# A decoder layer in fp32 on one core: FFN products in Strassen's seven-product form, all mixers first

## The chip, the cores and the metric

The kernel runs on one core of a Trainium2 chip. The metric is the device time of one execution in microseconds. The engines are PE (TensorE, matrix multiplication, with its weight loads PEld), DVE (VectorE), ACT (ScalarE), POOL (GpSimd) and SP (SyncE, which here issues nearly all transfers). Each works through its own instructions in order and waits on semaphores for the others.

## The reference

One layer on a sequence of 2048 tokens with 1024 features; hidden size of the FFN 4096; all float32. Cut to what matters:

```python
mod = silu(c) @ w_ada + b_ada                    # six vectors of 1024
shift1, scale1, gate1, shift2, scale2, gate2 = split(mod, 6)
h = rms_norm(x, g_mix) * (1 + scale1) + shift1
proj = h @ w_in                                  # gMLP u | v, then q, k, v: 1792 columns
out_a = chunked_sgu(gelu(proj[:, :1024]), w_spatial, b_spatial)      # chunks of 128 tokens
out_b = sliding_window_sink_attention(q, k, v, sinks, positions)     # window 128, 8 q and 2 kv heads
x = x + gate1 * (concat(out_a, out_b) @ w_out)
h2 = rms_norm(x, g_ffn) * (1 + scale2) + shift2
x = x + gate2 * (square(relu(h2 @ w_ff1)) @ w_ff2)
y = rms_norm(x, g_final)
```

## The kernel before

Activations are kept feature-major, 128 features on the partitions, and the sequence is cut into four slabs of T = 512 tokens. Every fp32 matrix product is made of three passes: each factor is split into a rounded part (`hi`, made by ACT, L253 for weights) and the rest (`lo`, made by DVE, L255), and `mm3` (L267 to L269) issues hi·hi, hi·lo and lo·hi into the same bank. Weights stream from DRAM in blocks of 128x1024: `w_next` keeps two blocks ahead in the order of the list `order`, each loaded by SP into one of three `raw` buffers.

A slab goes through `in_vu` (gMLP projection and gate), `in_qkv`, `attention`, `out_proj`, `ffn` and `final_norm`. `attention` has eight units (four blocks of 128 queries, two key heads), each in four stages: `stage_q` splits the queries; `stage_p` makes the scores (`sc`, L503) and their softmax in `pr` (DVE L510, L525, ACT's exponentials); `stage_t` transposes them (`tpp`, L534), splits them into `pc` (ACT L536, DVE L537) and masks them on POOL (`pp`, L541, L543); `stage_o` multiplies by the values (`ov`, L558) and copies out (`os`, ACT L561). `ffn` has eight chunks of 512 hidden features: four groups of 24 matmuls for the first product, then eight output groups of 12 for the second, added to `x2` (L634).

Generators set the program's order: `weave(main, side)` takes a step of `side` after each step or two of `main`. While slab s is in `ffn`, `attention` of slab s+1 and the statistics of slab s+2 are woven into it; `attention` of slab 0, which has no FFN before it, is skewed by stages and woven into the gMLP projections of slabs 0 and 1. The last slab's last chunk goes in halves of the columns, so that one half is normalised under the other. A scheduler then fixes each engine's order of instructions, with hand-written `issue_after` bounds.

The three places that decide what stands beside what:

```python
weave(chain(h_build(1, rb, hn), in_vu(1, hn, nxt)), zipped(att, ada), per=2)   # slab 0
...
side.append(attention(s + 1, nxt, False))
...
weave(main, chain(*side), every=2)                                             # main = ffn(s, st, h2)
```

## Time and profile before

| | |
|---|---|
| runs | 2143.32, 2145.67, 2146.58 us; median 2145.67 |
| span of the profiled execution | 2142.5 us (no other time is recorded for it) |
| PE busy | 2050.3 us, 9670 matmuls |
| DVE busy | 1296.7 us |
| ACT busy | 966.9 us |
| POOL busy | 256.7 us |
| transferred | 240.27 MB, mean 112 GB/s |

Busy times are sums over one profiled execution. PE's matmuls are pipelined, so that its busy time says when it was occupied and not that it ran at its peak; PEclk is the clock granted to TensorE, 1.00 being full speed. Marks of stages on PE: the first output projection begins at about 262 us, the first FFN at about 372 us.

### The profile page before, as it was taken

The page shows a single profiled execution, that of the slowest core. Times are in us where ns is not written, and L with a number is a line of the kernel's source. Part 1 is how long each engine was busy: PE and PEld are TensorE (multiplying, and loading weights), DVE is VectorE, ACT ScalarE, POOL GpSimd, SP SyncE. Part 2 cuts the span into 40 slices and gives each one's busy share as a digit, 9 for nine tenths or more (in the row PEclk, how much of TensorE's full clock was granted, in tenths as well). Part 3 has the DMA queues.
Part 4 walks back from the last instruction along what each step waited for, and adds up shares of the span by engine and source line. Part 5 has one row for each costly group of instructions (what it writes and reads, how often), then busy time and mean ns, then how long its engine had stood idle before and what let it go on. Part 6 is the DMA issues. An engine that isn't in the chain of part 4 may idle for free.

```text
span 2142.5 us, 25614 instructions
## 1 busy us (share of the span) xinstructions
PE 2050.3 (96%) x9670; PEld 1715.7 (80%) x9670; DVE 1296.7 (61%) x2068; ACT 966.9 (45%) x1642; POOL 256.7 (12%) x234
## 2 busy tenths in 40 slices
PE   5878898999999999999999999999999999999997
PEld 4777776888888888888887889888888888888886
DVE  8698768656563577655564577665554456444445
ACT  3555654544443443544453434444444243333334
POOL 5742253100000000100000000010000000000001
PEclk9978999999999999999999999999999999999998
DMA  9442172322233352322233362222222323322331
GB/s 333 151 145 64 55 245 93 107 89 80 98 128 99 111 186 89 99 89 89 89 103 113 99 206 89 89 89 98 82 93 92 118 94 123 113 99 89 99 98 60
DMA packets 81372, 240.27 MB, mean 112 GB/s; under 512 B 9904, under 2 KB 12080, under 8 KB 81248
## 3 DMA queue, kind: packets, MB, share of 16 engines
q1 hardware_dynamic: 80128, 237.91, 33.6%
q8 instruction: 76, 1.25, 0.2%
q0 software_dynamic: 1120, 0.72, 0.1%
q14 instruction: 48, 0.39, 0.1%
HBM read 230.01 MB, written 8.59 MB: 111 GB/s over the span
## 4 chain that ended last, share of the span: by engine, by line
PE 83%; DVE 7%; POOL 3%; ACT 2%; DMA 2%; issue 2%; SPq 0%; DVEq 0%; POOLq 0%; ACTq 0%
PE mm L267 26%; PE mm L269 25%; PE mm L268 25%; POOL acc L163 1%; PE sc L503 1%; PE ov L558 1%; PE mm L429 1%; PE mm L431 1%; PE mm L430 1%; DVE pr L510 1%; DVE wlo L255 1%; DMA xt<-in_x_dram 1%; DMA adap<-in_wada_dram 1%; PE tpp L534 1%; DMA raw<-in_win_dram 1%
## 5 line engine op out<-in xcount | busy, mean ns | idle before, releaser
L253 ACT ACTIVATE whi<-raw 128x1024 fp32r<-128x1024 f32 x344 | 363.9, 1059 | 819.3 <-PE mm L268 776.6
L255 DVE TENSOR_TENSOR wlo<-raw,whi 128x1024 fp32r<-128x1024 f32 x335 | 421.0, 1258 | 358.0 <-ACT whi L253 318.9
L267 PE MATMUL mm<-h,whi 128*128 128x512 f32 x1344 | 526.9, 394 | 12.0 <-ACT h L227 11.6
L269 PE MATMUL mm<-h,wlo 128*128 128x512 f32 x1344 | 526.8, 392 | 2.1 <-DVE wlo L255 1.6
L268 PE MATMUL mm<-h,whi 128*128 128x512 f32 x1344 | 526.1, 392 | 0.3 <-DVE h L228 0.3
L268 PE MATMUL mm<-a,whi 128*128 128x512 f32 (+1 forms) x1056 | 403.1, 384 | 0.0
L269 PE MATMUL mm<-a,wlo 128*128 128x512 f32 (+1 forms) x1056 | 402.6, 383 | 0.0
L267 PE MATMUL mm<-a,whi 128*128 128x512 f32 (+1 forms) x1056 | 395.5, 386 | 3.2 <-DVE x L634 3.1
L267 PEld LDWEIGHTS mm<-h,whi 128*128 128x128 f32 x1344 | 255.4, 190 | 65.0 <-ACT h L227 12.5
L269 PEld LDWEIGHTS mm<-h,wlo 128*128 128x128 f32 x1344 | 253.6, 189 | 55.4 <-DVE wlo L255 3.8
L268 PEld LDWEIGHTS mm<-h,whi 128*128 128x128 f32 x1344 | 254.0, 189 | 52.5 <-DVE h L228 1.3
L267 PEld LDWEIGHTS mm<-a,whi 128*128 128x128 f32 x1056 | 197.9, 188 | 47.7 <-DVE x L634 7.3
L269 PEld LDWEIGHTS mm<-a,wlo 128*128 128x128 f32 x1056 | 198.4, 188 | 39.0
L268 PEld LDWEIGHTS mm<-a,whi 128*128 128x128 f32 x1056 | 198.5, 188 | 37.5
L634 DVE SCALAR_TENSOR_TENSOR x<-mm,mod,x 128x512 f32<-128x512 f32 x192 | 140.0, 749 | 117.3 <-PE mm L269 116.6
L541 POOL TENSOR_SCALAR_AFFINE_SELECT pp<-pc 128x1024 fp32r<-128x1024 f32 x30 | 33.1, 1105 | 845.4 <-DVE pc L537 845.4
L615 DVE TENSOR_TENSOR a<-r,a 128x512 fp32r<-128x512 f32 x128 | 88.4, 692 | 63.5 <-ACT a L614 63.5
L199 POOL TENSOR_TENSOR rs<-ms,mhalf 128x4 f32<-128x4 f32 (+1 forms) x13 | 15.3, 1177 | 859.1 <-DVE ms L197 859.1
L429 PE MATMUL mm<-whi,h 128*128 128x256 f32 x256 | 75.4, 302 | 8.0 <-ACT vf L417 4.3
L614 ACT ACTIVATE a<-r 128x512 fp32r<-128x512 f32 x128 | 80.6, 631 | 5.2
L612 ACT ACTIVATE r<-r 128x512 f32<-128x512 f32 x128 | 80.8, 632 | 3.5
L634 DVE SCALAR_TENSOR_TENSOR x2p<-mm,mod,x2p 128x512 f32<-128x512 f32 x56 | 40.8, 749 | 67.0 <-PE mm L269 67.0
(185 smaller groups left out, 2482.5 us busy)
## 6 DMA issues: line engine op xcount, KB each, us to landing
raw<-in_w_dram SPq DMA_DIRECT2D x256, 512.0 KB, 3.5
raw<-in_win_dram SPq DMA_DIRECT2D x56, 512.0 KB, 4.2
xt<-in_x_dram SPq DMA_DIRECT2D x80, 256.0 KB, 3.1
raw<-in_wout_dram SPq DMA_DIRECT2D x32, 512.0 KB, 3.5
ada<-in_wada_dram SPq DMA_DIRECT2D x16, 512.0 KB, 8.1
adar<-in_wada_dram SPq DMA_DIRECT2D x32, 256.0 KB, 3.9
adap<-in_wada_dram SPq DMA_DIRECT2D x16, 512.0 KB, 5.1
out_dram<-y SPq DMA_DIRECT2D x24, 256.0 KB, 2.9
```

The source lines that it names most:

```text
L163: pool.tensor_tensor(out=acc, in0=acc, in1=raw, op=ALU.add)
L253: act.activation(out=hi, in_=raw, func=AF.Copy)
L255: ins = eng.tensor_tensor(out=lo, in0=raw, in1=hi, op=ALU.subtract)
L267: pe.matmul(out=out, lhsT=wh, rhs=h[:, 0], start=first, stop=False)
L268: pe.matmul(out=out, lhsT=wh, rhs=h[:, 1], start=False, stop=False)
L269: pe.matmul(out=out, lhsT=wl, rhs=h[:, 0], start=False, stop=last)
L429: pe.matmul(out=ov[:, b], lhsT=h[k][:, 0, cols], rhs=hi, start=k == 0, stop=False)
L541: pool.affine_select(out=pp, in_=pc, pattern=[[0, 8], [-1, P]], compare_op=ALU.is_gt, fill=0.0, base=0, channel_multiplier=1)
L612: act.activation(out=r, in_=r, func=AF.Square)
L614: act.activation(out=a[:, 0], in_=r, func=AF.Copy)
L615: dve.tensor_tensor(out=a[:, 1], in0=r, in1=a[:, 0], op=ALU.subtract)
L634: dve.scalar_tensor_tensor(out=x2[d], in0=outs[dd], scalar=mod[:, 5 * KT + d:5 * KT + d + 1], in1=x2[d], op0=ALU.mult, op1=ALU.add)
```

## The change

Two slabs form a pair. Each FFN product is a 2x2 block product, over halves of the features, halves of the hidden (or output) features, and the two slabs of the pair; it is made by seven block products in place of eight, with sums and differences of the blocks (`forms`) as factors.

- Order of the program: the mixers of all four slabs come first. `attention` of slabs 1 to 3, not skewed, is woven into the gMLP projection of the following slabs and into an output projection. Then `ffn_c(0)`, `ffn_d(0)`, `ffn_c(1)`, `ffn_d(1)`, for the first and the second product of pair 0 and pair 1.
- Mixer weights are split at their first use, and both parts are stored to DRAM (`w_keep`); later uses load both parts (`w_load`). `out_proj` stores its result `x2` to DRAM.
- `h2_build` makes seven forms of the FFN's input for each of four feature tiles: for pair 0 beside the last `out_proj`, for pair 1 a quarter after each of four products of `ffn_d(0)`.
- `ffn_c` has 16 steps of seven products of 12 matmul triples of K tiles (84 matmuls); DVE makes the weights' forms, and the hidden values' seven forms are stored to DRAM (`ad`). `w2_forms`, woven into `ffn_c(0)`, loads the second weight, makes its forms on POOL and stores them (`w2d`).
- `ffn_d` loads, for each of seven products and eight chunks, one block of `w2d` and one of `ad`, splits both and issues 24 matmuls into four banks.
- The last slab is no longer finished in halves. Pools change: eight `wk` tiles, a ring of four `wr`, a ring of four `xl`, 11 small `t2`, 58 `m2`.

```diff
 NEG = -1.0e30
-T2, T4 = 6, 23
+NT, NM, NWK, NWR, NXL = 11, 58, 8, 4, 4
 NPRE = 7
+NPAIR = NSLAB // 2
...
+    names = [("i", i) for i in (0, 1, 3, 4, 5, 6, 7)] + [("i", i) for i in range(8)]
+    names += [("o", i) for i in range(8)] + [("i", i) for i in range(8, 14)] + [("i", i) for i in range(8)]
+    names += [("o", i) for i in range(8)] + [("i", i) for i in range(8, 14)] + [("i", i) for i in range(4)]
+    names += [("i", i) for i in range(8, 14)] + [("o", i) for i in range(8)] + [("i", i) for i in range(4, 8)]
+    names += [("o", i) for i in range(8)]
+    pending = deque(names)
     ready = deque()
...
+    kept = {}
+    last_load = [None]
...
+    def w_split(key, big=False, eng=dve):
+        raw = wr("raw")
+        nc.sync.dma_start(out=raw, in_=(win if key[0] == "i" else wout)[key[1]])
...
+            act.activation(out=th, in_=r, func=AF.Copy)
+            ins = eng.tensor_tensor(out=tl, in0=r, in1=th, op=ALU.subtract)
...
+        w = Split(hi, lo)
+        w_keep(key, w)
+        return w
...
+    def w_keep(key, w):
+        n = D // len(w.hi)
+        kept[key] = [dram.tile([P, D], F32, name=f"k{key[0]}{key[1]}{q}", tag=f"k{key[0]}{key[1]}{q}") for q in "hl"]
+        for d, ts in zip(kept[key], (w.hi, w.lo)):
+            for i, t in enumerate(ts):
+                nc.sync.dma_start(out=d[:, i * n:(i + 1) * n], in_=t.bitcast(F32))
...
+    def w_load(key):
+        if key not in kept:
+            return w_split(key)
+        hi, lo = wk("whi"), wk("wlo")
+        for t, d in zip((hi, lo), kept[key]):
+            last_load[0] = nc.sync.dma_start(out=t.bitcast(F32), in_=d)
+        return Split([hi], [lo])
...
+    def mm3(out, wh, wl, h, first, last, more=False):
+
+        kw = dict(skip_group_check=True) if more else {}
+        pe.matmul(out=out, lhsT=wh, rhs=h[0], start=first, stop=False, **kw)
+        pe.matmul(out=out, lhsT=wh, rhs=h[1], start=False, stop=False, **kw)
+        pe.matmul(out=out, lhsT=wl, rhs=h[0], start=False, stop=last, **kw)
...
+            x2 = t2("x2")
...
+            nc.sync.dma_start(out=x2d[s][d], in_=x2)
+            yield
+        rb2[s] = stat.bcast(m2("rb2", F32))
+        yield
...
+    def token_forms(b11, b12, b21, b22):
...
+        t1, t_2, t4 = t2("wt"), t2("wt"), t2("wt")
+        dve.tensor_tensor(out=t1, in0=b12, in1=b11, op=ALU.subtract)
+        dve.tensor_tensor(out=t_2, in0=b22, in1=t1, op=ALU.subtract)
+        dve.tensor_tensor(out=b12, in0=b22, in1=b12, op=ALU.subtract)
+        dve.tensor_tensor(out=t4, in0=b21, in1=t_2, op=ALU.subtract)
+        return {1: b11, 6: t_2, 5: t1, 2: b21, 7: b12, 3: b22, 4: t4}
...
+    def h2_build(p, forms, ks):
...
+                    xt = sb.tile([P, T], F32, name="xt", tag="xl", bufs=NXL)
+                    nc.sync.dma_start(out=xt, in_=x2d[2 * p + t][kk])
+                    b = t2("hb")
+                    dve.scalar_tensor_tensor(out=b, in0=xt, scalar=gs[:, KT + kk:KT + kk + 1], in1=rb2[2 * p + t],
+                                             op0=ALU.mult, op1=ALU.mult)
+                    act.activation(out=b, in_=b, func=AF.Identity, bias=mod[:, 3 * KT + kk:3 * KT + kk + 1])
+                    bs_[half, t] = b
+            for i, f in token_forms(bs_[0, 0], bs_[0, 1], bs_[1, 0], bs_[1, 1]).items():
+                hi, lo = m2("hw"), m2("hw")
+                act.activation(out=hi, in_=f, func=AF.Copy)
+                dve.tensor_tensor(out=lo, in0=f, in1=hi, op=ALU.subtract)
+                forms.setdefault(i, []).append((hi, lo))
+            yield
...
+    def w2_forms():
+        for j in range(16):
+            c, e = divmod(j, 2)
...
+            def load(f0, d0):
+                t = sb.tile([P, T], F32, name="w2r", tag="xl", bufs=NXL)
+                for dp in range(2):
+                    o = t[:, dp * 2 * P:(dp + 1) * 2 * P].rearrange("p (a m) -> p a m", a=2)
+                    nc.sync.dma_start(out=o, in_=w2v[c, :, f0 + e, d0 + dp])
+                return t
...
+            def keep_form(i, t):
+                nc.sync.dma_start(out=w2d[i, c][:, e * T:(e + 1) * T], in_=t)
+
+            a11, a21, a22, a12 = load(0, 0), load(0, 2), load(2, 2), load(2, 0)
+            for i, t in ((1, a11), (2, a12), (4, a22)):
+                keep_form(i, t)
+            for i, o, x0_, x1_, op in ((5, a22, a21, a22, ALU.add), (7, a21, a11, a21, ALU.subtract),
+                                       (6, a11, a22, a11, ALU.subtract), (3, a12, a12, a11, ALU.subtract)):
+                pool.tensor_tensor(out=o, in0=x0_, in1=x1_, op=op)
+                keep_form(i, o)
                 yield
...
+    def ffn_c(p, forms):
+        for j in range(16):
+            c, e = divmod(j, 2)
+            r1, r2 = wr("r1"), wr("r2")
+            nc.sync.dma_start(out=r1, in_=w1[4 * c + e])
+            nc.sync.dma_start(out=r2, in_=w1[4 * c + 2 + e])
...
+            def split(src, name):
+                hi, lo = wk(name, [P, src.shape[1]]), wk(name, [P, src.shape[1]])
+                act.activation(out=hi, in_=src, func=AF.Copy)
+                dve.tensor_tensor(out=lo, in0=src, in1=hi, op=ALU.subtract)
+                return hi, lo
+
+            x1 = split(r1, "wa")
+            dve.tensor_tensor(out=s1, in0=r2[:, :T], in1=r2[:, T:], op=ALU.add)
+            dve.tensor_tensor(out=r2[:, :T], in0=r1[:, :T], in1=r2[:, :T], op=ALU.subtract)
+            dve.tensor_tensor(out=r1[:, :T], in0=s1, in1=r1[:, :T], op=ALU.subtract)
+            dve.tensor_tensor(out=r1[:, T:], in0=r1[:, T:], in1=r1[:, :T], op=ALU.subtract)
+            x2_ = split(r1, "wb")
+            x3 = split(s1, "wc")
+            x4 = split(r2, "wd")
+            wf = {1: (x1, 0), 6: (x2_, 0), 5: (x3, 0), 2: (x1, T), 7: (x4, 0), 3: (x2_, T), 4: (x4, T)}
...
+            def product(i, out, start):
+                (hi, lo), o = wf[i]
+                for k in range(4):
+                    cs = slice(o + k * P, o + (k + 1) * P)
+                    mm3(out, hi[:, cs], lo[:, cs], forms[i][k], start and k == 0, k == 3, not start)
...
+            x, y, z = bank("mm"), bank("sc"), bank("pt")
+            product(1, x, True)
+            p1 = t2("p1")
+            act.activation(out=p1, in_=x, func=AF.Copy)
+            yield
...
+            q = bank("mm")
+            product(7, q, True)
+            dve.tensor_tensor(out=w, in0=q, in1=w, op=ALU.add)
+            b22 = relu2(w)
+            yield
...
+            product(4, q, False)
+            dve.tensor_tensor(out=u, in0=q, in1=u, op=ALU.add)
+            b21 = relu2(u)
+            for i, f in token_forms(b11, b12, b21, b22).items():
+                c_last[0] = nc.sync.dma_start(out=ad[p, i, c][:, e], in_=f)
+            yield
...
+    def ffn_d(p, hook):
+        xs = {}
+        with tc.issue_after(c_last[0].ins):
+            for r, t in ((0, 0), (1, 1), (0, 1), (1, 0)):
+                for b in range(4):
+                    xt = m2("x3", F32)
+                    nc.sync.dma_start(out=xt, in_=x2d[2 * p + t][4 * r + b])
+                    xs[r, t, b] = xt
...
+        for n, (i, start) in enumerate(((1, True), (6, True), (2, False), (5, True), (7, True), (3, False), (4, False))):
+            if start:
+                sets[n % 2] = [bank(tag) for tag in BANKS[n % 2]]
+            outs = sets[n % 2]
+            for c in range(8):
+                wraw, araw = wr("w2w"), wr("aw", [P, 2, T])
+                nc.sync.dma_start(out=wraw, in_=w2d[i, c])
+                nc.sync.dma_start(out=araw, in_=ad[p, i, c])
+                wh, wl, ah, al = wk("w2h"), wk("w2l"), wk("ah", [P, 2, T]), wk("al", [P, 2, T])
+                act.activation(out=wh, in_=wraw, func=AF.Copy)
+                dve.tensor_tensor(out=wl, in0=wraw, in1=wh, op=ALU.subtract)
+                act.activation(out=ah, in_=araw, func=AF.Copy)
+                dve.tensor_tensor(out=al, in0=araw, in1=ah, op=ALU.subtract)
+                for e in range(2):
+                    for b in range(4):
+                        cs = slice(e * T + b * P, e * T + (b + 1) * P)
+                        mm3(outs[b], wh[:, cs], wl[:, cs], (ah[:, e], al[:, e]), start and c == 0 and e == 0,
+                            c == 7 and e == 1, not start)
+                yield
...
+            hook(i, last)
+            if i == 3:
+                final_norm(2 * p + 1, xs, 1, stats[1])
+        final_norm(2 * p, xs, 0, stats[0])
...
+    for s in range(1, NSLAB):
+        rope_load(s)
+        rn, hx = [], []
+        if s < NSLAB - 1:
+            weave(out_proj(s - 1, sts[s - 1]), chain(ada_rest(3 + s), x_stats(s + 1, rn)), per=2)
+            keep_halo(s - 1)
+            weave(in_qkv(s, hn, sts[s]), h_build(s + 1, rn, hx), per=2)
+            vu = in_vu(s + 1, hx, sts[s + 1])
+            att = attention(s, sts[s], False)
+            if s == NSLAB - 2:
+                weave(part(vu, 4), att, per=8)
+            else:
+                weave(vu, att, per=4)
+            hn = hx
+        else:
+            keep_halo(s - 1)
+            run(in_qkv(s, hn, sts[s]))
+            weave(chain(out_proj(s - 1, sts[s - 1]), vu), attention(s, sts[s], False), per=3)
...
+    with tc.issue_after(att_last[0].ins):
+        weave(out_proj(NSLAB - 1, sts[NSLAB - 1]), h2_build(0, forms, range(4)))
+    with tc.issue_after(last_load[0].ins):
+        weave(ffn_c(0, forms), w2_forms(), every=2)
...
+            todo = {6: (0,), 2: (1,), 5: (2,), 4: (3,)}
+
+            def hook(i, ins):
+                if i in todo:
+                    with tc.issue_after(ins.ins):
+                        run(h2_build(p + 1, nxt, todo[i]))
...
+        run(ffn_d(p, hook))
+        if p + 1 < NPAIR:
+            run(ffn_c(p + 1, nxt))
```

The order of the instructions on PE, at one unit of attention. Before, this is the transposes of one unit of slab 2 within `ffn`; 36 to 43 rows of FFN matmuls stand between the scores of a unit and its transposes, and 38 between these and `ov` (numbers behind the names tell buffers apart):

```order
L269 MATMUL mm_4763<-a_4678,wlo_4716 128x512
L534 MATMUL tpp_4746<-ident_66,pr_4681 128x128 x4
L267 MATMUL mm_4764<-a_4564,whi_4714 128x512
L268 MATMUL mm_4764<-a_4564,whi_4714 128x512
L269 MATMUL mm_4764<-a_4564,wlo_4716 128x512
L267 MATMUL mm_4764<-a_4601,whi_4714 128x512
L268 MATMUL mm_4764<-a_4601,whi_4714 128x512
L269 MATMUL mm_4764<-a_4601,wlo_4716 128x512
```

Now the same stages stand within the gMLP projection of the next slab; eight score rows of the next unit begin behind `ov`:

```order
L299 MATMUL mm_6062<-h_5185,whi_5855 128x512
L300 MATMUL mm_6062<-h_5186,whi_5855 128x512
L301 MATMUL mm_6062<-h_5185,wlo_5856 128x512
L583 MATMUL tpp_5596<-ident_66,pr_5565 128x128 x4
L608 MATMUL ov_5607<-pp_5604,vst_5274 128x512 x2
L608 MATMUL ov_5607<-pc_5601,vst_5274 128x512 x2
L552 MATMUL sc_5634<-kst_5232,qst_5623 128x256
```

What moved: the rows between transposes and `ov` are gone, and between scores and transposes few or none stand in most units. Over the program the rows of 128x512 matmuls between scores and transposes of the units of slab 1 are, in order, 42, 14, 20, 9, 3, 0, 6, 6; slab 2: 37, 0, 5, 0, 5, 0, 3 and 0; slab 3: 44, 2, 4, 25, 13, 4, none in the last but 14 and 6 inside its scores; between transposes and `ov` nearly none, but 25 once.

The order of transfers on SP. Before, in `ffn`, it is a plain stream of weights:

```order
L251 DMA raw_3305<-in_w2_dram 128x1024
L251 DMA raw_3342<-in_w1_dram 128x1024
L251 DMA raw_3407<-in_w1_dram 128x1024
L251 DMA raw_3444<-in_w1_dram 128x1024
L251 DMA raw_3492<-in_w1_dram 128x1024
L251 DMA raw_3529<-in_w2_dram 128x1024
L251 DMA raw_3582<-in_w2_dram 128x1024
```

Now, in `ffn_c(0)` (`r1`, `r2` are the first weight, `w2r` the second weight's quarters, `w2d` its forms going to DRAM, `ad` the hidden values' forms):

```order
L724 DMA r1_8962<-in_w1_dram 128x1024
L704 DMA w2d5_3_188<-w2r_9343 128x512
L725 DMA r2_8963<-in_w1_dram 128x1024
L704 DMA w2d7_3_204<-w2r_9340 128x512
L704 DMA w2d6_3_196<-w2r_9337 128x512
L700 DMA w2r_9519<-in_w2_dram 128x2x128 x2
L785 DMA ad0_1_2_211<-p1_8668 128x512
L704 DMA w2d3_3_172<-w2r_9346 128x512
L700 DMA w2r_9522<-in_w2_dram 128x2x128 x2
L700 DMA w2r_9525<-in_w2_dram 128x2x128 x2
L700 DMA w2r_9528<-in_w2_dram 128x2x128 x2
L785 DMA ad0_3_2_227<-w_8698 128x512
```

What moved: loads that PE's next step needs stand behind stores that wait for POOL and DVE, in one queue.

## Rows read from the trace of the kernel before

**Rows 1.** The page: busy time of the engines, and 40 slices of the span.

```profile
PE 2050.3 (96%) x9670; PEld 1715.7 (80%) x9670; DVE 1296.7 (61%) x2068; ACT 966.9 (45%) x1642; POOL 256.7 (12%) x234
...
PE   5878898999999999999999999999999999999997
...
PEclk9978999999999999999999999999999999999998
```

**Rows 2.** Windows: stretch, length, PE, PEld, DVE, ACT, POOL busy, PEclk, DMA share, GB/s.

```profile
30.00:60.00 30.00, 22.69 (x98) 17.84 (x96) 25.99 (x36) 4.28 (x6) 27.80 (x37) 0.88 0.87 319
...
150.00:200.00 50.00, 40.07 (x204) 36.06 (x205) 41.59 (x112) 26.03 (x74) 4.57 (x3) 0.73 0.17 53
...
900.00:1000.00 100.00, 99.66 (x457) 82.65 (x456) 58.56 (x115) 47.68 (x97) 7.51 (x6) 1.00 0.28 90
...
2100.00:2142.50 42.50, 29.04 (x220) 27.62 (x218) 23.82 (x54) 18.00 (x40) 6.56 (x8) 0.87 0.15 51
```

**Rows 3.** Timeline of PE, 907 to 918 us: start, duration, instruction.

```profile
907.16 1.12 PE L503 MATMUL sc<-kst,qst 128*128 128x256 f32 x8
908.12 0.40 PE L268 MATMUL mm<-h,whi 128*128 128x512 f32 x1
...
917.66 0.39 PE L268 MATMUL mm<-h,whi 128*128 128x512 f32 x1
917.89 0.60 PE L534 MATMUL tpp<-ident,pr 128*128 128x128 f32 x4
```

**Rows 4.** Timelines, 907 to 925 us: one attention unit on DVE, ACT and POOL.

```profile
912.39 0.69 DVE L525 TENSOR_TENSOR pr<-pr,den 128x512 f32<-128x512 f32 x1
...
919.57 0.58 ACT L536 ACTIVATE pc<-tpp 128x512 fp32r<-128x512 f32 x1
...
920.30 0.69 DVE L537 TENSOR_TENSOR pc<-tpp,pc 128x512 fp32r<-128x512 f32 x1
...
922.22 1.09 POOL L543 TENSOR_SCALAR_AFFINE_SELECT pc<-pc 128x1024 fp32r<-128x1024 f32 x1
```

**Rows 5.** Groups by line: busy us, mean ns of one, idle before.

```profile
L253 ACT ACTIVATE whi<-raw 128x1024 fp32r<-128x1024 f32 x344 | 363.9, 1059 | 819.3 <-PE mm L268 776.6 <-issue 25.2 <-DMA raw<-in_win_dram 14.6
L255 DVE TENSOR_TENSOR wlo<-raw,whi 128x1024 fp32r<-128x1024 f32 x335 | 421.0, 1258 | 358.0 <-ACT whi L253 318.9 <-PE ov L558 26.4 <-PE mm L269 4.5
...
L163 POOL TENSOR_TENSOR acc<-acc,adar 128x512 f32<-128x512 f32 x28 | 41.0, 1477 | 21.0 <-ACT adar L161 20.5
...
L561 ACT ACTIVATE os<-ov 64x512 f32<-64x512 f32 x32 | 19.0, 592 | 21.6 <-PE ov L558 21.3
...
L417 ACT ACT_TABLE_LOAD x7 | 9.0, 1283 | 14.5 <-PE mm L431 14.4
```

**Rows 6.** Timeline of PE in slab 0's attention, 159 to 171 us.

```profile
161.95 1.09 PE L534 MATMUL tpp<-ident,pr 128*128 128x128 f32 x4 [0.30 <-DVE pr L525]
...
166.10 1.05 PE L503 MATMUL sc<-kst,qst 128*128 128x256 f32 x4
```

**Rows 7.** Timeline of POOL, 85 to 105 us.

```profile
87.35 13.74 POOL L163 TENSOR_TENSOR acc<-acc,adar 128x512 f32<-128x512 f32 x8 [0.80 <-ACT adar L161]
```

**Rows 8.** Timeline of DVE, 85 to 105 us.

```profile
93.03 1.78 DVE L362 TENSOR_TENSOR qf<-qf,C_t 128x512 f32<-128x512 f32 x1
...
104.76 0.69 DVE L362 TENSOR_TENSOR qf<-qf,C_t 128x512 f32<-128x512 f32 x1
```

**Rows 9.** Timeline of SP's queue, 0 to 70 us.

```profile
27.33 6.74 SPq L121 DMA_DIRECT2D ada<-in_wada_dram  x8
```

**Rows 10.** The page's DMA issues: count, KB of one, median us to landing.

```profile
raw<-in_w_dram SPq DMA_DIRECT2D x256, 512.0 KB, 3.5
...
xt<-in_x_dram SPq DMA_DIRECT2D x80, 256.0 KB, 3.1
...
ada<-in_wada_dram SPq DMA_DIRECT2D x16, 512.0 KB, 8.1
...
out_dram<-y SPq DMA_DIRECT2D x24, 256.0 KB, 2.9
```

492 lines of the change are left out of this document (216 added, 276 removed).

## The prediction

> **What bounds the kernel now.** I read the page's busy shares first, then its slices, the windows by stage, and last single instructions on TensorE's timeline. TensorE is busy 2050.3 of 2142.5 us [rows 1], so at most 92 us are waits. The slices put these at the start: TensorE at 5 to 8 tenths in the first seven slices, 9 almost everywhere after them. The windows show the same: from 900 to 1000 us TensorE works 99.66 of 100 us at a granted clock of 1.00, while DVE is busy 58.56; in slab 0's mixer, 150 to 200 us, it works 40.07 of 50 at 0.73 [rows 2]. So the FFN stages, under which the mixers of slabs 1 to 3 are woven, are bound by TensorE, and a matmul taken out there is worth its interval. That interval is read from starts and not from the mean duration, since matmuls overlap: from 908.12 to 917.66 us there are 43 starts of 128x512 matmuls, 42 intervals in 9.54 us, 0.227 us each [rows 3].
>
> The same stretch shows what the FFN hides. One attention unit is (block, key head); it starts its scores at 907.16, its probabilities are normalised by DVE at 912.39 + 0.69 = 913.08 [rows 4], and its transposes come at 917.89 [rows 3], long after they could. From the scores' start to the earliest transpose is 5.9 us, in which TensorE has 0.9 us of its own scores; the other 5.0 us are DVE and ACT. Then the copy at 919.57, the low part at 920.30 and two masks on POOL, the last from 922.22 for 1.09, to 923.31: 3.7 us from transposes to `ov`, of which 3.5 are without TensorE work of the unit [rows 4]. These 8.5 us cost nothing in the kernel before, because other matmuls lie there.
>
> **What is removed.** FFN matmuls go from 6144 (4 slabs x 2 products x 32 x 8 tile pairs x 3) to 2 slab pairs x 2 products x 16 x 84 = 5376. 768 x 0.227 = **-174 us** at unchanged pace.
>
> **What is added, in order of the program.** (a) Attention of slabs 1 to 3, 24 units, has no FFN beside it. 24 x 8.5 = 204 us of latency, less what the new order leaves between the stages: counted row by row, the matmuls between scores and transposes, and between transposes and `ov`, capped at 5.0 and 3.5 us a unit, are worth 19, 9 and 24 us in slabs 1, 2 and 3. **+152**. TensorE's order shows the pattern: eight score rows, then directly the transposes, then directly `ov`. The bounds are 204 (no cover) and 96 (4 us a unit, if a DVE and an ACT without FFN work run the softmax faster).
>
> The Trainium skill, "Perfetto Trace Analysis", section Optimization Strategy, says that where the most contended engine changes over time, interleaving the regimes may help. This speaks against the change. Here the trace agrees, with 99.66 us of 100 on TensorE while attention runs beside it [rows 2]; taken to its end, with no cover left at all, the rule would make (a) 204 and the sum 2312.5.
>
> (b) Between units: after `ov` ACT copies `os` (592 ns), sometimes behind a table load (1283 ns) [rows 5], then the four query pieces of the next unit. Where the order leaves under 4 us of matmuls there, TensorE waits: 6, 8 and 3 us in slabs 1, 2, 3, **+17**.
>
> (c) The clock. In slab 0's mixer, where TensorE works in short pieces between waits, the granted clock is 0.73 [rows 2], and four transposes take 1.09 us and four score rows 1.05 [rows 6], against 0.60 and 1.12 for eight at full clock [rows 3]: the lower of the two levels, 1.2 GHz. The attention stages of slabs 1 to 3 will look like it. Bounds: 0, if the matmuls between keep the clock up, and some 130, if the three groups of 192 matmuls beside these attentions (two gMLP projections and an `out_proj`) all run at half pace (576 x 0.227). I take **+40**, a third: a unit's transposes cost 0.49 and its scores 0.98 us more at that level, with `ov` about 2, 48 us for 24 units, and part will be at the higher one.
>
> (d) The first FFN1 stage, `ffn_c(0)`, shares its time with `w2_forms`. TensorE needs 84 x 0.227 = 19.07 us a step, 305 us for 16. DVE has three low parts of 1258 ns [rows 5] and some 14 operations of 0.69 us [rows 4], 13.4 us; POOL four additions of about 1477 ns [rows 5], 5.9 us. A DVE operation took 1.78 us beside POOL's run of additions and 0.69 after it [rows 7, 8]: four such collisions make DVE 17.8 us, still under 19. Transfers are 5.77 MB a step, 92 MB in all; at the 319 GB/s of 30 to 60 us [rows 2] that is 289 us, under 305. SP issues 24 transfers a step; eight issues in a row took 6.74 us [rows 9], 0.84 each, so 20.2 us, 18 us too long over the stage. The chain of one set is four loads into a ring of four, POOL's 5.9, and the last store's landing before the next load: at the landings of 3.1 and 2.9 us [rows 10] about 12 us, no wait; at 8.1 us for each landing [rows 10] and 6.7 us of issue, 28.8 us, and because SP is one queue the next `r1` stands behind it: 16 x 28.8 - 305 = 156. So 0 to 156; I take **+35**, SP's 18 and as much again for late first sets, because the landings of most rows are nearer 3 than 8 us.
>
> (e) Transfers beside `out_proj`(0) and the next queries: the new stores (high and low of each first weight, 8.4 MB for `wout`) make 31.5 MB, 99 us at 319 GB/s against 336 x 0.227 = 76 us of matmuls; one slab later 27.3 MB, 86 against 76. 0 to 33, **+15**. (f) Stores of the first seven weights, 7.3 MB or 23 us, in a stretch whose transfers already run at 0.87 [rows 2]: 0 to 23, **+12**. (g) Slab 1's gate weights come split from DRAM: eight low parts of 1.26 us [rows 5] leave a stretch where DVE is 41.59 of 50 busy [rows 2]: 0 to -15, **-8**. (h) `h2_build(0)` beside the last `out_proj`: DVE 54 us (60 + 16 operations of about 0.7) against 192 x 0.227 = 44: **+10**, 0 to 12. (i) Between the first `ffn_d` and the second `ffn_c` the last quarter of the forms is built only after the last evacuation: load 3.1, four additions, split, some 15 us before the first product can end: **+15**, 8 to 25. (j) The end: before, the last chunk runs in halves of the columns, and TensorE is idle 13.5 us of the last 42.5 [rows 2]; now a whole slab's norm follows the last product: four evacuations with their squares, POOL's power, the spread, eight outputs at about 0.7 us and a store of 2.9 [rows 10], some 17 us: **+4**, 0 to 10. The rest of `ffn_d` I cost at nothing: a chunk needs 2.1 us of ACT and 2.5 of DVE under 24 x 0.227 = 5.45 us of matmuls, and the mixing of the products lies under the next product's eight chunks, since two sets of four banks alternate. Without that cover each of 14 products would show about 4 us.
>
> Sum: 2142.5 - 174 + 152 + 17 + 40 + 35 + 15 + 12 - 8 + 10 + 15 + 4 = 2260.5. That is against the profiled execution's span; the median of the runs shown, 2145.67, is 3 us above it, so 2264.
>
> **Rivals.** *A, the forecast*: attention laid bare costs more than Strassen saves; 2264, by its unknowns 2180 to 2330. Chance 0.61. *B, the forms of w2 bind the first FFN stage*: SP, in order, waits for stores to land and holds `r1` back; 28.8 us a step, 2260.5 - 35 + 156 + 3 = 2385, and milder forms between. For it speaks 8.1 us on the busiest landings, against it 3.5 on the weight stream [rows 10]. 0.18. *C, `ffn_d` waits for its loads*: ring of four, so two chunks in flight; 8.1 us landing, two ACT and two DVE operations of 1.06 and 1.26 [rows 5] make 12.7 us per two chunks, 6.35 against 5.45, times 112: +101, 2365. Against it speaks that the stage moves only 1.05 MB per 5.45 us, 192 GB/s, below the 319 seen. 0.08. *D, the other side*: the attention waits shrink. Break-even is where (a) falls to 174 - 83 = 91 with (b) and (c) at nothing, 3.8 us a unit (83 being the terms d to j); at 2 us a unit (DVE and ACT free of FFN work, transposes ahead by the order's matmuls) it is 2142.5 - 174 + 83 + 48 + 3 = 2103. Against it: the 5.9 us chain is mostly one operation after the other, not queueing. 0.10. *E, the two balance*, 0.03. That the matmuls are not saved can't be: the order counts 5376.
>
> Measurements of this kernel tell about 0.2% from no change. B and C are slower as well, so faster 0.10, same 0.03, slower 0.87. The range drops D and E's 0.13 and the tail of the rest: from 2175, just under A's own, to 2390, over B's 2385.
>
> **What would show it.** FFN matmuls 5376; the first FFN product near 970 us, with TensorE waiting after each block of scores for DVE's `pr` and after the transposes for POOL's mask, about 6 us a unit; a granted clock clearly below 1 between roughly 280 and 900 us; `ffn_c(0)` near 340 us, the other three FFN stages near 305 each with a clock of 1; a gap of 15 us ahead of the second `ffn_c`. It is wrong if TensorE's idle time in the attention stages is under 100 us, if `ffn_c(0)` passes 400 us, or if matmuls in FFN stages start further apart than 0.227 us.

## The result, and the profile after

The changed kernel takes 2516.71 us (median of four runs, 2514.85 to 2525.88); the kernel before took 2146.05 us beside it. The ratio is 1.174, 95% interval 1.1719 to 1.1761. The direction was forecast, the size was not: 2264 us was predicted, in a range up to 2390.

The page's busy times and slices after the change (its span is 2516.8 us), against [rows 1]:

```profile
PE 2052.2 (82%) x8852; PEld 1655.5 (66%) x8852; DVE 1392.8 (55%) x2342; ACT 992.6 (39%) x1750; POOL 306.9 (12%) x286
...
PE   5959787567855866788877889999788889999997
...
PEclk9969898778865986899888999999899999999998
```

TensorE has fewer matmuls and is busy as long as before, so each lasts longer in the mean, and it is now idle 465 us of the span where it was idle 92. The slices put the waits at two places: the attention stages of slabs 1 to 3 (slices 7 to 16), as expected, and, in the second half of the program, the two `ffn_c` stages, where 9 was expected and mostly 7 and 8 stand. Windows by stage, columns as in [rows 2]; the stages are attention of slabs 1, 2 and 3 with the matmuls woven into it (lines 1, 3, 4; line 2 is what stands between two of them), then `ffn_c(0)`, `ffn_d(0)`, `ffn_c(1)`, `ffn_d(1)`:

```profile
382.50:549.50 167.00, 97.60 (x416) 74.74 (x415) 64.81 (x218) 64.38 (x180) 17.46 (x16) 0.73 0.14 48
549.50:662.00 112.50, 95.37 (x447) 79.92 (x448) 48.50 (x92) 37.03 (x63) 24.01 (x24) 0.89 0.73 253
662.00:808.00 146.00, 76.09 (x268) 53.95 (x266) 56.53 (x201) 50.01 (x164) 17.46 (x16) 0.62 0.12 44
...
838.90:990.00 151.10, 105.45 (x470) 84.49 (x469) 67.51 (x222) 48.32 (x160) 18.49 (x17) 0.78 0.30 101
...
1054.60:1468.20 413.60, 335.37 (x1344) 264.39 (x1343) 237.04 (x277) 144.87 (x208) 98.76 (x65) 0.92 0.66 224
1468.20:1790.30 322.10, 313.00 (x1368) 257.78 (x1367) 198.18 (x220) 142.93 (x167) 1.02 (x1) 0.99 0.65 214
1790.30:2182.70 392.40, 332.42 (x1344) 259.90 (x1343) 220.10 (x301) 151.26 (x220) 1.39 (x1) 0.94 0.35 122
2182.70:2498.40 315.70, 311.35 (x1368) 256.68 (x1366) 169.80 (x174) 123.47 (x133) 1.01 (x1) 0.99 0.61 202
```

A way to account for it, used below: of each stage, TensorE's idle time is summed over the gaps ahead of its matmuls ("waits"); the work is 0.227 us for each 512 columns [rows 3]; what is left of the stage's length are matmuls that run longer than that, for a lower clock or a pipeline that starts anew ("long matmuls"). Over the whole program waits grew by 371 us and long matmuls by 178, and the work fell by 174, as forecast: about 374 us, which is also the difference of the spans, because the long matmuls are by definition what is left.

The attention stages lose 183 us to waits and 100 to long matmuls. One unit of slab 2, all engines:

```profile
718.13 2.04 PE L552 MATMUL sc<-kst,qst 128*128 128x256 f32 x8 [1.81 <-DVE qst L531]
...
724.29 0.69 DVE L574 TENSOR_TENSOR pr<-pr,den 128x512 f32<-128x512 f32 x1
725.13 1.09 PE L583 MATMUL tpp<-ident,pr 128*128 128x128 f32 x4 [4.95 <-DVE pr L574]
...
728.79 1.22 PE L608 MATMUL ov<-pp,vst 128*128 128x512 f32 x2 [2.57 <-POOL pp L590]
...
733.76 0.79 PE L299 MATMUL mm<-h,whi 128*128 128x512 f32 x1 [2.59 <-ACT u L456]
```

These are the predicted waits at the predicted places: 4.95 us for the softmax (5.0 was forecast), 2.57 for the mask (3.5: `ov` starts with the first of POOL's two masks), and 2.59 behind `ov` for ACT, with a table load and a gelu in its queue. The four transposes take 1.09 us, as those of [rows 6].

What was not forecast is `ffn_c`. In the second pair nothing stands beside it, and yet its steps take 23.7 us where 84 matmuls need 19.07. One step's turn, all engines (the `wd` matmul is the last of the old step; `u` is its last product's sum, `p` the copy of the next step's first product, `r` and `wb` the next step's weights):

```profile
1903.89 0.39 PE L301 MATMUL mm<-hw,wd 128*128 128x512 f32 x1
1904.31 0.69 DVE L782 TENSOR_TENSOR u<-mm,u 128x512 f32<-128x512 f32 x1
...
1905.04 0.63 ACT L751 ACTIVATE u<-u 128x512 f32<-128x512 f32 x1 [1.42 <-DVE u L782]
...
1905.70 0.63 ACT L752 ACTIVATE u<-u 128x512 f32<-128x512 f32 x1
...
1906.23 0.58 ACT L758 ACTIVATE p<-mm 128x512 f32<-128x512 f32 x1
1906.36 0.69 DVE L664 TENSOR_TENSOR wt<-u,wt 128x512 f32<-128x512 f32 x1 [0.16 <-ACT u L752]
...
1906.87 0.50 PE L299 MATMUL mm<-hw,wa 128*128 128x512 f32 x1 [2.59 <-ACT p L758]
...
1909.14 0.69 DVE L738 TENSOR_TENSOR r<-r 128x512 f32<-128x512 f32 x1
...
1909.87 1.06 ACT L730 ACTIVATE wb<-r 128x1024 fp32r<-128x1024 f32 x1 [3.05 <-DVE r L738]
...
1910.97 0.50 PE L299 MATMUL mm<-hw,wb 128*128 128x512 f32 x1 [1.09 <-ACT wb L730]
```

The next step's first product was finished by 1899, but its copy `p` stands in ACT's queue behind the old step's last square, which waits for the old step's last product; the next matmuls add into the bank that `p` is copied from, so TensorE waits 2.59 us. Then DVE makes the next weights' forms only behind the old step's sums (L664), and `wb` comes 4 us after that wait; here TensorE waits 1.09 us more for it. That second wait stands in six steps. In the last eight there is none: the granted clock falls behind the first wait, and the product between the waits ends only when `wb` is there:

```profile
2025.29 0.80 PE L299 MATMUL mm<-hw,wa 128*128 128x512 f32 x1 [2.59 <-ACT p L758]
2025.89 0.63 PE L300 MATMUL mm<-hw,wa 128*128 128x512 f32 x1
2026.31 0.63 PE L301 MATMUL mm<-hw,wa 128*128 128x512 f32 x1
...
2029.59 0.40 PE L299 MATMUL mm<-hw,wb 128*128 128x512 f32 x1
...
2025.30:2028.60 3.30, 3.30 (x8) 2.63 (x9) 2.85 (x5) 0.31 (x1) 0.00 (x0) 0.53 0.72 271
1906.90:1910.00 3.10, 2.98 (x12) 2.14 (x12) 2.83 (x5) 0.14 (x1) 0.00 (x0) 1.00 0.77 287
```

The last two lines are windows behind the first wait, in such a step (clock 0.53) and in the step shown above (1.00). Both kinds of step take 23.7 us, so it is the chain through ACT and DVE that sets the length and not TensorE's own pace; in the mean of ten steps the 4.6 us are 3.0 of waits and 1.6 of long matmuls. Two queues that are in order, ACT's busy 39% and DVE's 56% of the stage, hold the engine that bounds it.

### The profile page after: what moved, and what is told of

The parts are those of the page before. It is cut to its first block, busy times and chain, and to the rows that moved or that the text cites. A ratio compares the mean times of both kernels' runs of the same rounds, so it can differ in the third digit from the quotient of the medians.

```text
span 2516.8 us, 26096 instructions
## 1 busy us (share of the span) xinstructions
PE 2052.2 (82%) x8852; PEld 1655.5 (66%) x8852; DVE 1392.8 (55%) x2342; ACT 992.6 (39%) x1750; POOL 306.9 (12%) x286
## 4 chain that ended last, share of the span: by engine, by line
PE 40%; DVE 5%; DMA 3%; ACT 2%; issue 1%; SPq 1%; POOL 1%; POOLq 0%; DVEq 0%; ACTq 0%
PE mm L299 13%; PE mm L301 13%; PE mm L300 13%; DMA x<-x2d 1%; DMA w2d<-w2r 1%; DVE u L782 1%; ACT u L751 1%; DVE x L807 1%; ACT wb L730 1%; POOL w2r L711 1%; DMA aw<-ad 1%; SPq L700 0%; DVE r L736 0%; DVE s L735 0%; DVE hb L676 0%
## 5 line engine op out<-in xcount | busy, mean ns | idle before, releaser
L300 PE MATMUL mm<-al,w2h 128*128 128x512 f32 x896 | 351.7, 393 | 6.2 <-DVE al L827 6.1
L301 PE MATMUL mm<-ah,w2l 128*128 128x512 f32 x896 | 351.3, 392 | 0.0
L299 PE MATMUL mm<-ah,w2h 128*128 128x512 f32 x896 | 296.5, 391 | 7.2 <-ACT ah L826 7.2
L299 PE MATMUL mm<-hw,wa 128*128 128x512 f32 x256 | 117.6, 459 | 104.1 <-ACT p L758 101.5
L300 PEld LDWEIGHTS mm<-al,w2h 128*128 128x128 f32 x896 | 169.6, 189 | 43.7 <-DVE al L827 8.3
L299 PEld LDWEIGHTS mm<-ah,w2h 128*128 128x128 f32 x896 | 168.9, 189 | 43.1 <-ACT ah L826 8.1
L301 PEld LDWEIGHTS mm<-ah,w2l 128*128 128x128 f32 x896 | 169.5, 189 | 35.2
L299 PE MATMUL mm<-h,whi 128*128 128x512 f32 x320 | 136.3, 436 | 23.2 <-ACT u L456 7.8
L301 PE MATMUL mm<-h,wlo 128*128 128x512 f32 x320 | 134.4, 421 | 4.9 <-POOL wlo L269 4.7
L827 DVE TENSOR_TENSOR al<-aw,ah 128x1024 fp32r<-128x1024 f32 x112 | 136.5, 1219 | 1.2 <-ACT ah L826 1.1
L300 PE MATMUL mm<-h,whi 128*128 128x512 f32 x320 | 134.0, 419 | 0.0
L299 PE MATMUL mm<-hw,wb 128*128 128x512 f32 x256 | 103.9, 406 | 21.9 <-ACT wb L730 21.9
L300 PE MATMUL mm<-hw,wa 128*128 128x512 f32 x256 | 112.8, 441 | 1.4 <-DVE hw L683 1.4
L301 PE MATMUL mm<-hw,wa 128*128 128x512 f32 x256 | 112.0, 438 | 0.0
L301 PE MATMUL mm<-hw,wb 128*128 128x512 f32 x256 | 103.6, 405 | 0.1
L300 PE MATMUL mm<-hw,wb 128*128 128x512 f32 x256 | 101.3, 396 | 0.0
```

Source lines behind the costliest of these rows:

```text
L299: pe.matmul(out=out, lhsT=wh, rhs=h[0], start=first, stop=False, **kw)
L300: pe.matmul(out=out, lhsT=wh, rhs=h[1], start=False, stop=False, **kw)
L301: pe.matmul(out=out, lhsT=wl, rhs=h[0], start=False, stop=last, **kw)
L827: dve.tensor_tensor(out=al, in0=araw, in1=ah, op=ALU.subtract)
```

## The experiments

Each is told with its edit, and with the text written before it ran. Times are of a single run each where no interval is given; the kernel before took 2145.3 us beside the first four, 2146.0 beside the next four, and 2145.4 to 2146.3 (medians) beside the others.

**Order of the queues in the first FFN product.** The evacuation of a step's last product becomes a function, which the next step calls behind its copy `p1`:

```diff
-            act.activation(out=p1, in_=x, func=AF.Copy)
+            early = act.activation(out=p1, in_=x, func=AF.Copy)
+            if tail:
+                with tc.issue_after(early.ins):
+                    tail()
```

> In the first FFN product the last evacuation of a step (DVE u, ACT's square, the sums and stores) is queued behind ACT's copy p1 of the next step. Two theories of the steady step of 23.7 us, where 84 matmuls need 19.07: (1) TensorE waits for ACT's copy p1 because ACT has the old step's evacuation ahead of it; then the 2.6 us wait goes, steps come to 21.1 us, the two stages lose about 80 us and the kernel is near 2437 us. (2) One chain limits the step: product 4, DVE's evacuation, ACT's square, DVE's sums, and only then DVE's forms of the next weights and ACT's split wb. Then the wait only moves from p1 to wb, steps stay at 23.5 to 24 us and the kernel stays within 15 us of 2517.

Measured: 2411.3 us; the steps of `ffn_c(1)` are 20.2 us. The wait for `p` is gone, and that for `wb` did not take its place: 0.29 us for `wb` and 0.31 for `wc` are left. Theory (1) is nearer, and the gain is more than it said: in the mean of ten steps waits fall from 3.0 to 0.6 us and long matmuls from 1.6 to 0.6. The second edit puts DVE's forms ahead as well:

```diff
-                with tc.issue_after(early.ins):
+                with tc.issue_after(early.ins), tc.issue_after(formed.ins):
```

> As the run with the copy first, and DVE's four forms of the next step's weights also stand ahead of the old step's evacuation. By theory (2), the chain through DVE, both waits go: steps of 19.1 to 19.8 us, the second of the two stages falls from 392 to about 325 us, the first from 414 to about 345, the kernel to about 2380. By the rival, that transfers in SP's one queue (r1, r2 behind stores) hold the step, nothing changes: steps of 23.7 us, 2517.

Measured: 2397.7 us. The steps of `ffn_c(1)` are 19.1 us, to the tenth what the matmuls need. Its windows, `ffn_c(0)` and the second pair's stage without its first 25 us:

```profile
1053.00:1413.00 360.00, 322.75 (x1344) 254.78 (x1343) 262.59 (x277) 142.19 (x209) 108.46 (x65) 0.97 0.76 256
1762.00:2061.30 299.30, 298.30 (x1308) 244.28 (x1309) 193.09 (x263) 139.95 (x204) 0.00 (x0) 1.00 0.45 152
```

TensorE is now busy 298.3 of 299.3 us in the second pair. `ffn_c(0)`, with the second weight's forms beside it, is not repaired: 365 us from its first matmul to its last (the window's 360 leave out the 5 that overlap `ffn_d`).

**The mixers first, and Strassen, each by itself.** The kernel after with the FFN of before behind its mixers:

```diff
-        weave(ffn_c(0, forms), w2_forms(), every=2)
...
+    for s in range(NSLAB):
+        main = ffn_plain(s, h2s[s])
```

> Mixers first as in the changed kernel, but both FFN products in eight block products per slab, weights streamed and hidden values kept in SBUF, as before (6144 matmuls). If Strassen's saving is eaten by its own waits (the FFN stages of the changed kernel last 1444 us, 6144 matmuls at 0.227 us need 1395), this one is faster than the changed kernel: 1055 + 1395 + about 30 = 2480 us. If the form keeps its 174 us and the loss is all in the mixers, this one is near 2517 + 174 = 2690.

Measured: 2468.4 us, 48 less than the changed kernel. The seven-product form as it stands loses more than its 174 us of work. And the kernel before with nothing but its attention laid bare:

```diff
-            side.append(attention(s + 1, nxt, False))
+            run(attention(s + 1, nxt, False))
```

> The kernel before, with the attention of slabs 1 to 3 issued ahead of each FFN stage and not woven into it; all else as it was. If laying attention bare is the main loss, 24 units of about 14.8 us (scores, 5 us of softmax, transposes, 2.6 us to the values, values, 1.8 us to the next scores, TensorE at its lower clock) less some 56 us of their matmuls that were paid before give about +300: 2445 us. If the scheduler still finds FFN matmuls to put between, or the loss in the changed kernel is mostly transfers, it is under +100: below 2250.

Measured: 2449.9 us, +305. Its attention of slab 1, and the FFN stage behind it:

```profile
372.00:494.30 122.30, 46.18 (x142) 29.48 (x142) 54.04 (x174) 38.96 (x128) 17.46 (x16) 0.53 0.04 13
494.30:973.50 479.20, 477.19 (x2209) 397.27 (x2209) 252.83 (x328) 187.87 (x257) 8.17 (x11) 0.99 0.35 109
```

Eight units take 122 us, 15.3 each, at a granted clock of 0.53, near the lower of the two levels (1.2 of 2.4 GHz), while the FFN stage runs at 0.99. That is the price of the cover which the change gave up.

**The second weight's forms**, on the version with copy and forms first. They are left out:

```diff
-        weave(ffn_c(0, forms), w2_forms(), every=2)
+        run(ffn_c(0, forms))
...
-                nc.sync.dma_start(out=wraw, in_=w2d[i, c])
+                nc.sync.dma_start(out=wraw, in_=w2[4 * c + i % 4])
```

> On the version with copy and forms first (2398 us): the forms of the second weight are left out, neither made nor stored, and the second FFN product reads plain blocks of that weight in their place. With them the first FFN stage took 365 us in steps of 20 to 24 us. If the forms' transfers and POOL work beside it make that, the steps come to 19.1 us as in the second pair and the stage to about 312: the kernel near 2345. If the stage is late for another cause (stores of hidden values, first steps), it stays within 10 us of 2398.

Measured: 2354.5 us, and `ffn_c(0)` takes 315 us in steps of 19.1 after the first. The forms cost 50 us there.

**The clock in the attention stages.** 20 matmuls on constants, of no use to the result, between scores and transposes, and 10 between transposes and values:

```diff
+            if s > 0:
+                with tc.issue_after(scored.ins):
+                    filler(tp, 20)
             for j in range(4):
```

> The changed kernel, with 20 matmuls on constants between scores and transposes and 10 between transposes and values in each attention unit of slabs 1 to 3, of no use to the result, which keep TensorE at work while it waits for DVE and POOL. Counted from the trace, these stages lose 183 us to waits and 102 us to matmuls that run longer than at full clock. If the 102 us are the lower clock that follows waits, the granted clock in the three stages rises from 0.62 to 0.78 to over 0.9 and, since about 30 us of the new matmuls fall where there was no wait, the kernel comes to about 2450. If the long matmuls have another cause, the new ones only add: 2540.

Measured: 2519.0 us, no change. The three stages:

```profile
381.60:547.80 166.20, 139.74 (x656) 111.89 (x654) 63.81 (x216) 62.13 (x176) 17.47 (x16) 0.92 0.14 49
661.00:812.00 151.00, 126.88 (x516) 97.62 (x516) 59.56 (x210) 51.59 (x169) 17.46 (x16) 0.88 0.12 43
840.00:994.00 154.00, 142.90 (x695) 116.07 (x695) 66.85 (x221) 47.65 (x159) 18.49 (x17) 0.96 0.29 97
```

The granted clock rises from 0.73, 0.62 and 0.78 to 0.92, 0.88 and 0.96, and long matmuls fall from 100 to 66 us; the fillers took 163 us (720 at 0.227), of which 120 fell into waits and 43 did not. The clock is part of the loss, as theory one said, but a clock bought with matmuls gave back no more here than they cost. Neither time that was forecast came.

**Overlap of the units.** The attention of slabs 1 to 3 in the skewed order that slab 0 has:

```diff
-            att = attention(s, sts[s], False)
+            att = attention(s, sts[s], True)
```

> The changed kernel with the attention of slabs 1 to 3 in skewed order: scores of the next unit ahead of the transposes of this one. TensorE's order now has the scores of the next unit or two in the 5 us of softmax. If the waits are each unit's own chain, laid end to end, half of the 183 us go and some clock with them: about 2420. If DVE and ACT are the limit of the stages (a unit needs some 6 us of DVE), or the ring of four buffers for probabilities, the waits only move: 2500 to 2530.

Measured: 2370.4 us, 146 less, more than either theory said. The stages:

```profile
384.30:498.60 114.30, 80.17 (x416) 65.84 (x414) 68.43 (x213) 59.03 (x170) 17.89 (x16) 0.86 0.20 70
611.70:709.30 97.60, 62.52 (x272) 48.11 (x270) 60.90 (x197) 48.64 (x159) 17.96 (x16) 0.79 0.20 71
741.90:847.30 105.40, 90.78 (x472) 77.33 (x471) 74.69 (x218) 45.86 (x155) 19.75 (x17) 0.91 0.42 145
```

Waits fall from 183 to 84 us and long matmuls from 100 to 53. So most of the waits were each unit's chain laid end to end, and DVE, busy 68 of 114 us in the first stage, was no limit. What holds the 84 us that are left was not taken apart.

**The copies in DRAM.** Each use of a mixer weight loads the raw block and splits it:

```diff
-        w = Split(hi, lo)
-        w_keep(key, w)
-        return w
+        return Split(hi, lo)
...
+        return w_split(key)
```

> The changed kernel without the DRAM copies of the split mixer weights: each use loads the raw block and splits it on ACT and DVE, as before the change. If transfers hold the prologue and the two stages of output projection and queries (119 and 113 us with 90 and 83 us of matmuls), these lose 20 to 40 us and the kernel comes to about 2490. If the splits cost more in the attention stages, whose DVE and ACT chains TensorE waits for, than the transfers save, it is 2520 to 2540.

Measured: 2528.1 us, 11 more. The two projection stages got shorter (127.5 to 114.9 and 114.3 to 108.9 us; transfers of 281 and 250 GB/s became 180 and 185), so the copies, their stores and their loads of twice the size, did cost about 18 us there; the attention of slab 1 between the two got 13 shorter as well. The prologue, up to the first output projection, is 16 longer, and the way from the attention of slab 2 to the FFN 25.

**The repairs together.** Skewed attention, and copy and forms first:

> The two repairs together: attention of slabs 1 to 3 skewed, and copy and forms first in the first FFN product. If they act on separate stages, their gains add: 2517 - 146 - 119 = 2252. If the first FFN stage, begun earlier, meets transfers that were done before, less: up to 2280.

Measured: 2220.2 us, 32 better than the sum: `ffn_c(0)` takes 337 us here and not 365, with the same work in it, only otherwise timed (more on this below). Then the second weight's forms were moved from `ffn_c(0)` to the attention:

```diff
+        for n, _ in enumerate(attention(s, sts[s], True)):
+            if n % 3 < 2:
+                next(w2g, None)
+            yield
```

> As skew_forms, with the forms of the second weight made beside the attention of slabs 1 to 3 (two steps of them to three of attention), where transfers took 0.12 to 0.30 of the time, and not beside the first FFN stage. If that stage's 20 to 24 us steps were the forms' doing, it falls to about 315 us and the kernel to about 2210. If POOL's additions now delay the masks that TensorE waits for (64 additions of 1.5 us, two or three to a unit), the attention stages give back 20 to 50 us: 2230 to 2260. Either way it stays above the kernel before: waits and clock in the mixers still cost over 150 us and the seven-product form saves 174.

Measured: 2236.8 us, ratio 1.0435 (1.0417 to 1.0452). `ffn_c(0)` falls to 315 us, and the three attention stages give back 42 (114 to 132, 98 to 111, 105 to 117). Next, on skew_forms, the output projection of the slab before is put into the attention of slabs 1 and 2:

```diff
-            weave(out_proj(s - 1, sts[s - 1]), chain(ada_rest(3 + s), x_stats(s + 1, rn)), per=2)
...
+            for _ in out_proj(s - 1, sts[s - 1]):
+                run(part(att, 2))
```

> As skew_forms, and in slabs 1 and 2 the queries' projection comes first and the output projection of the slab before is woven with the attention, ahead of the gMLP projection, so that some 200 more matmuls stand between the stages of each attention (as they already do in slab 3, where waits are 17 us and the long matmuls 14). If what is left of the loss in slabs 1 and 2 (69 us of waits, 38 us of long matmuls) is for want of matmuls to put there, half of it goes, and part of the 37 us of waits in the two projection stages: about 2165. If these stages are held by DVE and by transfers (282 GB/s in the first), the waits move and it stays between 2200 and 2230.

Measured: 2181.9 us, ratio 1.0182 (1.0145 to 1.0219). The FFN begins at 830 us and not at 902, as the first theory wanted, but `ffn_c(0)` now takes 371. With these mixers and the plain FFN:

> The mixers of skew_forms_out, and after them both FFN products in eight block products per slab as in plain_ffn. It tells what the seven-product form is worth once the mixers are repaired: in skew_forms_out the FFN takes 1350 us from its first product to the end, 6144 matmuls at 0.227 us and plain_ffn's ends 1405. If the form's saving is what is left after its own waits, this one is at 830 + 1405 + 3 = 2238 us, 56 slower than skew_forms_out; if the FFN stages share a loss with the mixers, nearer 2182.

Measured: 2246.4 us. So the seven-product form is worth 65 us once the queues are in order, of the 174 us of work that it saves.

**What makes `ffn_c(0)` long.** The version skew_forms_out, with loads and stores of the forms on POOL's queue, then with the stores alone (the line of the stores, which both have):

```diff
-                nc.sync.dma_start(out=w2d[i, c][:, e * T:(e + 1) * T], in_=t)
+                nc.gpsimd.dma_start(out=w2d[i, c][:, e * T:(e + 1) * T], in_=t)
```

> As skew_forms_out, with the loads and stores of the second weight's forms issued on POOL's own queue and not on SP's. There the first FFN stage took 371 us, 56 over its limit without these forms, and SP waited 77 us of it for POOL's additions, with the next step's weights and the hidden values' stores behind. If SP's order makes the excess, the stage falls to 315 to 330 us and the kernel to 2125 to 2140, below the kernel before (2145). If it is DVE, held up beside POOL's additions, or the transfers' rate, the stage stays over 355 and the kernel over 2165; POOL issuing 240 transfers itself may add to that.

> As out_pool_queue, but only the stores of the forms go to POOL's queue; their loads stay on SP, where they wait for a free buffer. If SP's waits for POOL's additions were the excess, this gives most of it: 2135 to 2150. If the loads' waits for buffers are what holds SP then, it stays near 2175.

Measured: 2221.4 us, ratio 1.0341 (1.0324 to 1.0358), and `ffn_c(0)` 412 us, with everything on POOL's queue; 2172.5 us and 362 us with the stores alone. SP waits 77 us of the stage for POOL's additions in skew_forms_out, and taking the stores out of its queue gave 9 us. That does not clear SP's queue: with the stores alone moved, its loads wait for buffers, as the last sentence of the second text had it, and with everything moved a new delay comes in on DVE. SP's waits in `ffn_c(0)` of the second (us in total, times, longest):

```profile
SPq L700 <- DMA w2d<-w2r: 119.5, 43, 8.5
```

DVE's groups in `ffn_c(0)` of the first (mean ns of one behind the busy us):

```profile
L737 DVE TENSOR_TENSOR r<-r,r 128x512 f32<-128x512 f32 x16 | 33.9, 2118 | 0.6
L738 DVE TENSOR_TENSOR r<-s,r 128x512 f32<-128x512 f32 x16 | 32.8, 2047 | 0.5
...
L782 DVE TENSOR_TENSOR b<-mm,u 128x512 f32<-128x512 f32 x15 | 10.4, 692 | 64.2 <-PE mm L301 64.2
```

These two of the four forms of the weights last three times their 0.69 us, while the sum that reads a PSUM bank (`mm`) keeps its 692 ns. In the changed kernel itself, `ffn_c(0)`, where POOL adds:

```profile
L731 DVE TENSOR_TENSOR wd<-r,wd 128x1024 fp32r<-128x1024 f32 x16 | 24.9, 1559 | 0.0
...
L663 DVE TENSOR_TENSOR b<-w,b 128x512 f32<-128x512 f32 x15 | 14.5, 969 | 0.0
...
L778 DVE TENSOR_TENSOR b<-mm,u 128x512 f32<-128x512 f32 x15 | 10.4, 692 | 67.1 <-PE mm L301 67.1
```

In `ffn_c(1)`, without POOL, the first two are 1219 and 685 ns and the third 691. The Trainium skill, "SBUF — State Buffer", section "SBUF: two separate sides", states that DVE and POOL share a pair of ports by an exclusive lock, which a DVE operation with two SBUF inputs needs against a POOL operation that reads SBUF. The traces agree, by up to 1.1 us an operation in the changed kernel and up to 1.6 with POOL also issuing transfers, and none with a PSUM input was longer. These operations are on the path. In the version with copy and forms first, 25 of the 37 us that TensorE waits in `ffn_c(0)` end at a DVE split that lasts 1.7 or 2.3 us, where one alone lasts 0.69 (128x512) or 1.22 (128x1024). Two lines of TensorE's waits there, and the two DVE groups:

```profile
PE mm L301 <- DVE wc L732: 21.5, 13, 2.1
PE mm L301 <- DVE wb L732: 7.1, 9, 1.1
...
L732 DVE TENSOR_TENSOR wb<-r,wb 128x1024 fp32r<-128x1024 f32 x16 | 29.4, 1838 | 1.1 <-ACT wb L731 1.1
L732 DVE TENSOR_TENSOR wc<-s,wc 128x512 fp32r<-128x512 f32 x16 | 21.6, 1349 | 0.0
```

DVE is busy 266 us in this stage. In skew_forms, where the same operations take the stage 337 us and not 365, it is busy 215: fewer of them met an addition. To take POOL out, the additions go to DVE, on skew_forms_out and on the version with copy and forms first:

```diff
-                pool.tensor_tensor(out=o, in0=x0_, in1=x1_, op=op)
+                dve.tensor_tensor(out=o, in0=x0_, in1=x1_, op=op)
```

> As skew_forms_out (SP's queue as it was), with the four additions of the second weight's forms on DVE and not on POOL. In the runs so far DVE operations of two SBUF inputs last up to 1.09 us longer in the first FFN stage where POOL adds, those with a PSUM input never, and the stage's length goes with DVE's busy time a step: 14.3 us and 337, 15.9 and 362, 17.3 and 371, 18.1 and 412. If these collisions are the excess, DVE is 13.3 + 4 x 0.69 = 16.1 us a step and undisturbed, the stage takes 315 to 335 us, the kernel 2125 to 2145: level with the kernel before or just under. If DVE's sheer load or waits for the loads are, 16.1 us give about 365 again: 2175.

> The same on the version with copy and forms first but mixers as changed (2398 us, first FFN stage 365 us). By the collisions: the stage at 315 to 335 us, the kernel at 2350 to 2370. By DVE's load: 2398 again.

Measured: 2171.0 us, ratio 1.0124 (1.0105 to 1.0144), and 2387.3 us; `ffn_c(0)` takes 360 and 358 us. DVE's groups in `ffn_c(0)` of the first:

```profile
L711 DVE TENSOR_TENSOR w2r<-w2r 128x512 f32<-128x512 f32 x64 | 43.9, 686 | 37.5 <-DMA w2d<-w2r 33.2 <-DMA ad<-p 3.0 <-issue 0.9
...
L663 DVE TENSOR_TENSOR b<-w,b 128x512 f32<-128x512 f32 x16 | 10.9, 683 | 0.0
```

All collisions are gone, and most of the excess is not: the additions overwrite blocks whose stores must land first, and now DVE's queue waits 33 us for these landings, with the weights' forms behind. So the forms cost `ffn_c(0)` 20 to 100 us (337 to 412 us against 315), and with collisions gone another queue's waits take their place. What they cost by themselves, and how much of the excess they made in the changed kernel, where most of TensorE's waits end at `p`, is not shown.

No version is faster than the kernel before; the nearest is 1.2% slower.

## Why the prediction was wrong, step by step

- **What is removed, -174:** right, -174 in the matmuls' records.
- **(a) and (b), attention laid bare, +169:** 183 us of waits. The unit's chain and its places were right, the sum to 14 us, in part by luck: the waits for softmax and mask are 142 us where (a) had 152, and those between units 35 where (b) had 17. before_bare (+305 where +300 was expected) shows the mechanism by itself.
- **(c), the clock, +40:** 100 us of long matmuls in these stages, too small by 60 though inside its bounds. The step took a third of the bound because part would run at the higher level. By the clock's records in the trace, which stand at 0.5 or 1.0, the lower level held for 266 of these stages' 461 us, and 86 of the 100 us are of matmuls issued in that time. In kept_warm these are 33 us, at the price of its fillers.
- **(d) and the stages of the second pair, +35 and nothing:** here the prediction failed. "TensorE needs 84 x 0.227 = 19.07 us a step" is true, and "the other three FFN stages near 305" was read from it; what DVE and POOL need in sum was held against 19 us (ACT was not counted), but not the order in which DVE's and ACT's queues serve two steps. A step took 23.7 us. `ffn_c(1)` lost 90 us where 15 stood for (i), `ffn_c(0)` 111 where 35 stood. c_forms_first takes the two queued pieces out of the way and gets 19.1 us a step in the second pair; about 21 us at that stage's start are left there, which is (i) itself. `ffn_c(0)` took 419 us from its first matmul to its last, over the 400 that the prediction had named as a sign that it is wrong. The prediction weighed the order of TensorE's and SP's instructions, and not that of ACT's and DVE's, which holds it.
- **(d), the forms of the second weight:** +50 us by f_no_w2_forms, with the queues repaired, against 35. The mechanism was put into SP's queue and transfers. The collisions with POOL were priced at 17.8 us of DVE a step and dismissed since that is under 19; c_forms_first shows that they do count where they fall on the chain that a step waits for.
- **(e), stores beside the output projections, +15:** the two stages hold 67 us of waits and long matmuls, where the one such stage of before held 27, counted from its first `out_proj` matmul (at 248.2 us, with the bulk of them from 262) to 372; without the copies 18 us go.
- **(f) to (j):** (f) and (g) together 5 us instead of 4; (h) 21 instead of 10; the `ffn_d` stages and the end 18 more than thought, with three waits of 3 to 4 us: near the start of each `ffn_d` for a load that lands late (3.47 and 3.77 us), and once for a split that stands in DVE's queue behind evacuations and `h2_build` (3.16).
- **Rivals:** B named the right stage and 2385 us, but by SP's queue, and the loss of `ffn_c(1)`, where no forms are made, is outside it. C did not come, but for its two late loads: the `ffn_d` stages take 322 and 316 us against 305. D's mechanism, less wait per unit, is what skewed brings, but it was not in the kernel.

In sum, the terms missed by: (a), (b) +14, (c) +60, (d) +76, (e) +25, (h) +11, (i) +75, the rest about -5 (among it +18 for `ffn_d` and the end, and -26 for small losses in the FFN stages of before, which the sum had carried over): 256 us, the span's 2516.8 less 2260.5.

## What to carry to other kernels

Taking work off the bounding engine pays only if what stood beside that work still has cover: here 768 matmuls saved 174 us, and the attention that the FFN had hidden cost 283. For a loop of several short products, write down the order of each in-order queue across two turns of the loop before summing busy times: an engine that is idle half of the time can still hold the loop if next turn's first piece stands behind this turn's last. Where waits must remain, overlap two chains (skewing gave 146 us) rather than fill the gaps.
